# A two-layer decoder trunk on one core: the relative bias table is built in the first mixer instead of the first feed-forward

## The chip, the cores and the metric

The kernel runs on one core of one Trainium2 chip. The time is device microseconds (us) from the launch to the end on that core; a median over several runs is compared with a median. Beside the timed runs one execution was taken with the hardware profiler, and all rows below are from that one.

## The reference

The program computes two layers of a decoder on 256 tokens of width 1024. Each layer is a half-step feed-forward, a mixer and a second half-step feed-forward; every sub-layer is modulated by shift, scale and gate vectors made from a conditioning vector `c` and the weights `w_ada`.

```python
for l in range(DEPTH):                                   # DEPTH = 2
    mod = (silu(c) @ w_ada[l] + b_ada[l]).reshape(...)   # 9 vectors of 1024 per layer
    h = pre(x, 0)                                        # RMS norm, scale, shift
    x = x + 0.5 * mod[:, 0, 2] * swiglu(h, w_ffn_gate[l, 0], w_ffn_up[l, 0], w_ffn_down[l, 0])
    h = pre(x, 1)
    q_sb, ..., g_swa = split(h @ w_in[l])
    o_sb  = stick_breaking_mixer(q_sb, k_sb, v_sb)       # uses no bias
    o_dil = dilated_mixer(q_dil, k_dil, v_dil, rel_bias) # scores + band_bias(rel_bias)
    o_swa = swa_mixer(q_swa, k_swa, v_swa, rel_bias, sinks[l])
    merged = sigmoid(g_sb) * (o_sb @ w_br_sb[l]) + ...   # three gated branches
    x = x + mod[:, 1, 2] * (merged @ w_out[l])
    h = pre(x, 2)
    x = x + 0.5 * mod[:, 2, 2] * swiglu(h, ...)
return rmsnorm(x, final_gain)
```

The part that matters here is the bias: for each of 12 softmax heads, each query row needs the bias of its distance to every key, masked where the head may not look. The table `rel_bias` is 32 buckets by 12 heads and is the same for both layers.

## The kernel before

The stages run in the order FFN 0, mixer 1, FFN 2, FFN 3, mixer 4, FFN 5. All weights stream from HBM once. Work goes in **units**, each a 128x1024 piece of weights (half of a 1 MB `raw` tile). For each unit ScalarE (ACT) rounds the piece to a high part (`wH`, line 150), VectorE (DVE) makes the low part by subtracting (`wL`, line 158), and TensorE (PE) multiplies with both parts. `feed` keeps this splitting five units ahead of PE (`AHEAD = 5`, six buffers of each part, three `raw` buffers). An FFN has 44 units of gate and up products (FFN 0 begins with 12 in another form, so 32 in its loop; tile `pf`), then 22 units of down products (`pd`), the last four in pieces. After them come the gate and residual on DVE (`y`, `x`, lines 535 and 536), a norm, and transposes (`psn`) for the next stage. A mixer has 6 units of value products (`pv`), 14 units of query and key products (`pq`), then gates and branches (`pg`, `pb`), then the output rows.

Between the units a second stream runs: 512 KB pieces of `w_ada` (tile `ada`, two buffers) are multiplied and summed on DVE (`acc`, line 283), a few per unit by a written table of paces. Nothing is reordered by a scheduler: every engine runs its instructions in the order in which the code issues them, and so does each queue. All weight loads are issued on SP's queue (`q1` in the profile) in program order; each waits there for its buffer.

Attention in the mixer is interleaved with units. The stick-breaking pairs (no bias) run beside the query and key units: scores on PE (`pz`) behind unit 5, `z` on DVE, three activations into `e`, `e` again on DVE beside unit 7 (line 986), cumulated sums on PE (`pc`) behind unit 9, `z` minus them on DVE (line 995), an exponential, and the product `po` behind unit 11. The softmax heads start with the first gate unit; there the bias tile `Tm` is added to the scores on DVE (line 1054).

The bias is made in three helpers: four small loads on SP's queue; one small fp32 product, a masked sum and two DMAs on POOL's queue (`q0` in the profile); and one load per mixer, which reads the repeated rows at a slant so that each query row gets its own shift.

```python
def bias_loads(self):                      # line 413
    nc.sync.dma_start(oh, a["onehot"]); nc.sync.dma_start(mk, a["dmask"])
    nc.sync.dma_start(rb, a["rel_bias"]); nc.sync.dma_start(self.sink, a["sinks"]...)
def bias_table(self):                      # line 425
    nc.tensor.matmul(p[:NHEAD, :NDIST], rb, oh, start=True, stop=True)          # psr
    nc.vector.tensor_tensor(mk, p[:NHEAD, :NDIST], mk, op=ALU.add)
    nc.gpsimd.dma_start(row, mk)                                                # 12x383 to DRAM
    nc.gpsimd.dma_start(self.scr, row.unsqueeze(1).to_broadcast([NHEAD, P, NDIST]))
def load_bias(self, T):                    # line 435
    nc.gpsimd.dma_start(T, src)                                                 # scr to SBUF
```

Below, "the copy" is the second DMA of `bias_table` (`scr<-row`, DRAM to DRAM, 1536 rows of 383 floats).

Of the kernel before, what the change touches and what calls it, by code (L numbers as in the profile page):

```python
# [89 lines left out]
class Trunk:  # L90
# [704 lines left out]
    def run_ffn(self, plan, early=None):  # L795
        s = plan["s"]
        if s:
            self.alloc_ffn(s)
        if s:
            us = plan["in"][:2]  # L800
            for u in us:
                self.feed()
                self.ada_tick()
                u.pe(u, "high")
            for u in us:
                u.pe(u, "low")
            self.done(2)
        for i, u in enumerate(plan["in"]):
            if i > 1 or s == 0:
                self.step(u)  # L810
            if s == 0 and i == 8:
                self.bias_loads()
            if s == 0 and i == 16:
                self.bias_table()
        self.flush()
        self.run_rows(plan["out"], s, self.ffH, self.ffL, early)

# [320 lines left out]
    def run_mixer(self, plan):  # L1138
        s, l = plan["s"], plan["l"]
        nc = self.nc  # L1140
        bigA = self.sp.tile([P, 5376], F32, tag="bigA", name=f"qkv{s}", bufs=1)
        self.qk = bigA[:, 0:3840].rearrange("p (b n) -> p b n", n=S)
        self.v = bigA[:, 3840:5376].rearrange("p (t n) -> p t n", t=2)
        bigB = self.sp.tile([P, 5120], F32, tag="bigB", name=f"Tm{s}", bufs=1)
        self.T = bigB[:, 0:3072].rearrange("p (h n) -> p h n", n=256)
        self.m = bigB[:, 3072:5120].rearrange("p (b n) -> p b n", n=S)
        self.oH = self.sp.tile([P, 6, S], F32R, tag="oA", name=f"oH{s}", bufs=1)
        self.oL = self.sp.tile([P, 6, S], F32R, tag="oB", name=f"oL{s}", bufs=1)
        self.load_bias(self.T)

        pv = plan["pv"]
        for i, u in enumerate(plan["v"]):
            self.feed()
            self.ada_tick()
            self.v_pe(i, u, pv, (1,) if i < 2 else (0, 1), "high" if i < 2 else "all")
            if i == 1:
                for k in range(2):
                    self.v_pe(k, plan["v"][k], pv, (1,), "low")
                self.done(2)
            elif i > 1:  # L1160
                self.done()
        for t in range(2):
            self.v_post(t, pv[t])

        sb, soft = self.sb_stages(s), self.soft_stages(s, l)
        when = {}

        def at(part, fns, arg, units):
            for fn, i in zip(fns, units):
                if fn:  # L1170
                    when.setdefault((part, i), []).append((fn, arg))

        at("qk", sb, 0, (5, 6, 7, 9, 10, 11))
        at("qk", sb, 1, (7, 8, 9, 11, 12, 13))
        at("br", soft[:4], ("dil", 0), (0, 1, 2, 4))
        at("br", soft[:4], ("dil", 1), (2, 3, 4, 6))
        at("br", soft[4:], "dil", (8,))
        at("br", soft[:4], ("swa", 0), (7, 8, 9, 11))
        at("br", soft[:4], ("swa", 1), (10, 11, 12, 15))
        at("br", soft[4:], "swa", (17,))  # L1180
        for i, u in enumerate(plan["qk"]):
            self.step(u)
            if i == 4:
                nc.scalar.preload_act_table_set("natural_log_exp_and_others")
            for fn, arg in when.get(("qk", i), ()):
                fn(arg)
        nc.scalar.preload_act_table_set("exp_and_others")
        for i, u in enumerate(sum(plan["br"], [])):
            if i == len(plan["br"][0]) + len(plan["br"][1]):
                mm = self.sp.tile([P, 2, KB, S], F32R, tag="bigA", name=f"mHL{s}", bufs=1)  # L1190
                self.mH, self.mL = mm[:, 0], mm[:, 1]
            self.step(u)
            for fn, arg in when.get(("br", i), ()):
                fn(arg)
        self.flush()
        self.run_rows(plan["out"], s, self.mH, self.mL)
# [154 lines left out]
```

## Time and profile before

| | |
|---|---|
| median of 3 runs | 1212.38 us (1212.31 to 1213.13) |
| the profiled execution | 1215.12 us, of which its span is 1213.4 us |
| PE busy | 1181.0 us, 97% of the span |
| DVE busy | 837.3 us, 69% |
| ACT busy | 616.0 us, 51% |
| mean granted PE clock | 0.992 of full speed |
| DMA | 287.55 MB, mean 237 GB/s |

A busy share is a mean over stages with different limits, and PE's ends are modelled, so a stretch can count as busy although matmuls in it stand further apart. What a stage is bound by is read from the chain of work that ended last and from the waits of that stage.

### The profile page before, as it was taken

The numbers are of one execution on the slowest core, as the hardware profiler recorded it, in microseconds if no ns is written. First come the engines' busy times: TensorE is split into PE (matmuls) and PEld (weight loads), VectorE is DVE, ScalarE is ACT, GpSimd is POOL, SyncE is SP. The second block draws the span as 40 slices with busy tenths as digits, with TensorE's granted clock in tenths as the row PEclk, the third lists the DMA queues.
The fourth block names the chain that finished last, engine by engine and source line by source line (L and its number), as shares of the span: only waits on it lengthen the run. The fifth ranks groups of instructions, "written<-read, shape, count | busy, mean of one in ns | idle before, by whom it ended". The sixth has DMA issues, their size and how long they took to land.

```text
span 1213.4 us, 21101 instructions
## 1 busy us (share of the span) xinstructions
PE 1181.0 (97%) x8765; PEld 1102.9 (91%) x8765; DVE 837.3 (69%) x1087; ACT 616.0 (51%) x953; POOL 19.0 (2%) x38
## 2 busy tenths in 40 slices
PE   6999998899999999999999999999999999999997
PEld 5999986699999899999889999889999998999986
DVE  3677575878889888766577666567766788555544
ACT  5555343556555475444365444346655456444432
POOL 1000000000000000000000000000000000000000
PEclk9999999899999999999999999999999999999999
DMA  9999889698769959876738676748743584556550
GB/s 318 313 303 332 272 308 318 211 314 271 253 230 314 319 176 326 263 243 242 261 112 298 219 242 226 258 157 291 264 149 113 186 276 147 190 178 197 180 176 35
DMA packets 189671, 287.55 MB, mean 237 GB/s; under 512 B 6806, under 2 KB 155496, under 8 KB 189576
## 3 DMA queue, kind: packets, MB, share of 16 engines
q1 hardware_dynamic: 187656, 279.88, 68.8%
q0 software_dynamic: 1776, 6.14, 1.7%
q8 instruction: 68, 1.11, 0.4%
q14 instruction: 27, 0.22, 0.1%
q10 hardware_dynamic: 144, 0.20, 0.0%
HBM read 285.12 MB, written 3.42 MB: 238 GB/s over the span
## 4 chain that ended last, share of the span: by engine, by line
PE 85%; DMA 6%; DVE 3%; ACT 2%; issue 2%; POOL 1%; SPq 0%; POOLq 0%; ACTq 0%; DVEq 0%
PE pf L594 37%; PE pd L706 16%; PE pg L594 12%; PE pq L594 7%; DMA ada<-in_w_ada 5%; PE pb L594 3%; PE pf L624 3%; PE pv L942 2%; DVE acc L283 1%; DVE wL L158 1%; PE adaf L212 1%; DMA first<-in_w_ada 1%; PE psn L488 1%; ACT wH L150 1%; ACT jk L452 0%
## 5 line engine op out<-in xcount | busy, mean ns | idle before, releaser
L158 DVE TENSOR_TENSOR wL<-raw,wH 128x1024 fp32r<-128x1024 f32 (+1 forms) x384 | 461.8, 1211 | 224.8 <-ACT wH L150 224.3
L150 ACT CAST wH<-raw 128x1024 fp32r<-128x1024 f32 (+1 forms) x384 | 393.1, 1040 | 244.5 <-PE pd L706 90.1
L594 PE MATMUL pf<-hH,wH 128*128 128x256 f32 x1312 | 324.5, 285 | 0.4 <-DVE hH L505 0.4
L594 PE MATMUL pf<-hH,wL 128*128 128x256 f32 x1312 | 323.5, 284 | 0.0
L594 PEld LDWEIGHTS pf<-hH,wH 128*128 128x128 f32 x1312 | 253.1, 193 | 1.7 <-issue 0.9
L594 PEld LDWEIGHTS pf<-hH,wL 128*128 128x128 f32 x1312 | 253.5, 193 | 0.2 <-issue 0.2
L594 PE MATMUL pf<-hL,wH 128*128 128x256 f32 x1312 | 183.8, 283 | 0.0
L283 DVE SCALAR_TENSOR_TENSOR acc<-ada,sc,acc 128x1024 f32<-128x1024 f32 x112 | 143.4, 1280 | 40.6 <-DMA ada<-in_w_ada 40.6
L594 PEld LDWEIGHTS pf<-hL,wH 128*128 128x128 f32 x1312 | 169.1, 192 | 0.0
L706 PE MATMUL pd<-wL,ffH 128*128 128x512 f32 x336 | 132.7, 395 | 5.1 <-DVE wL L158 5.1
L706 PE MATMUL pd<-wH,ffH 128*128 128x512 f32 x336 | 132.5, 394 | 0.0
L706 PE MATMUL pd<-wH,ffL 128*128 128x512 f32 x336 | 132.2, 393 | 0.0
L594 PE MATMUL pg<-hH,wH 128*128 128x256 f32 x384 | 96.0, 288 | 0.0
L594 PE MATMUL pg<-hH,wL 128*128 128x256 f32 x384 | 94.0, 283 | 0.0
L652 ACT ACTIVATE sil<-pf 128x256 f32<-128x256 f32 x88 | 33.3, 382 | 98.4 <-PE pf L594 98.4
L706 PEld LDWEIGHTS pd<-wL,ffH 128*128 128x128 f32 x336 | 63.9, 190 | 19.3 <-DVE wL L158 6.2
L706 PEld LDWEIGHTS pd<-wH,ffH 128*128 128x128 f32 x336 | 63.9, 190 | 14.0 <-issue 0.8
L706 PEld LDWEIGHTS pd<-wH,ffL 128*128 128x128 f32 x336 | 64.0, 190 | 13.2
L594 PEld LDWEIGHTS pg<-hH,wH 128*128 128x128 f32 x384 | 73.5, 191 | 2.3 <-issue 0.9
L594 PEld LDWEIGHTS pg<-hH,wL 128*128 128x128 f32 x384 | 73.6, 192 | 0.0
L653 DVE TENSOR_TENSOR f<-pf,sil 128x256 f32<-128x256 f32 x88 | 36.9, 422 | 33.9 <-ACT sil L652 33.9
L594 PE MATMUL pq<-hH,wH 128*128 128x256 f32 x224 | 55.8, 287 | 0.0
(215 smaller groups left out, 1437.2 us busy)
## 6 DMA issues: line engine op xcount, KB each, us to landing
ada<-in_w_ada SPq DMA_DIRECT2D x128, 512.0 KB, 5.4
raw<-in_w_ffn_down SPq DMA_DIRECT2D x44, 1024.0 KB, 4.8
raw<-in_w_in SPq DMA_DIRECT2D x42, 1024.0 KB, 6.1
raw<-in_w_ffn_gate SPq DMA_DIRECT2D x41, 1024.0 KB, 6.1
raw<-in_w_ffn_up SPq DMA_DIRECT2D x41, 1024.0 KB, 5.8
first<-in_w_ada SPq DMA_DIRECT2D x32, 256.0 KB, 6.0
raw<-in_w_out SPq DMA_DIRECT2D x8, 1024.0 KB, 7.1
raw<-in_w_ffn_gate SPq DMA_DIRECT2D x12, 256.0 KB, 6.0
```

The costliest lines, as they stand in the source:

```text
L150: nc.scalar.copy(u.H, u.view(self.raw_tiles[u.raw]))
L158: nc.vector.tensor_tensor(u.L, u.view(self.raw_tiles[u.raw]), u.H, op=ALU.subtract)
L212: self.nc.tensor.matmul(self.first_ps[q % 2][32 * i:32 * i + 32, 0:P], w, src[:, i * P:(i + 1) * P], start=kb in (0, None), stop=kb == KB - 1)
L283: self.nc.vector.scalar_tensor_tensor(acc, src, sc, acc, ALU.mult, ALU.add)
L488: self.nc.tensor.transpose(p[:, i * P:(i + 1) * P], xn[:, fb * P:(fb + 1) * P], self.ident)
L594: nc.tensor.matmul(out, w[:, kb, cs], x[:, kb, :], start=i == 0, stop=i == n - 1)
L624: self.nc.tensor.matmul(ps[fb][:, S * up:S * up + S], w[:, 2 * k + up, b * P:(b + 1) * P], x[:, 2 * q + k, :], start=q == 0 and not up and ...
L652: nc.scalar.activation(sil, p[:, :S], AF.Silu)
L653: nc.vector.tensor_tensor(f32, p[:, S:], sil, op=ALU.mult)
L706: self.nc.tensor.matmul(out, x[:, kb, sl], w[:, 0, hs], start=first and i == 0, stop=last and i == 2)
L942: self.nc.tensor.matmul(out, x[:, 4 * (i % 2) + k, sl], w[:, k, :], start=i % 2 == 0 and j == 0, stop=i % 2 == 1 and j == n - 1)
```

## The change

The four small loads and the table are no longer issued behind units 8 and 16 of FFN 0's loop. In the first mixer the loads are issued at its start in the place of `load_bias`, and the table and then `load_bias` behind the last value unit (i = 5). The second mixer is as before. No instruction is added or left out.

```diff
@@ run_ffn
         for i, u in enumerate(plan["in"]):
             if i > 1 or s == 0:
                 self.step(u)
-            if s == 0 and i == 8:
-                self.bias_loads()
-            if s == 0 and i == 16:
-                self.bias_table()
         self.flush()
@@ run_mixer
-        self.load_bias(self.T)
+        if s == 1:
+            self.bias_loads()
+        else:
+            self.load_bias(self.T)
 
         pv = plan["pv"]
         for i, u in enumerate(plan["v"]):
...
                 self.done(2)
             elif i > 1:
                 self.done()
+            if s == 1 and i == 5:
+                self.bias_table()
+                self.load_bias(self.T)
         for t in range(2):
             self.v_post(t, pv[t])
```

On SP's queue of the kernel before, the four small loads stand between the weight loads of FFN 0 (`in_w_ffn_gate`, `in_w_ffn_up`).

```order
L133 DMA raw_1066<-in_w_ffn_up 128x8x256
L260 DMA ada_1069<-in_w_ada 128x1024
L418 DMA oh<-in_onehot 32x383
L419 DMA mk<-in_dmask 12x383
L420 DMA rb<-in_rel_bias 32x12
L422 DMA sink<-in_sinks 128x12
L133 DMA raw_1139<-in_w_ffn_gate 128x8x256
```

In the changed kernel they stand behind the third weight load of the query and key units (`in_w_in`).

```order
L133 DMA raw_2255<-in_w_in 128x8x256
L133 DMA raw_2457<-in_w_in 128x8x256
L133 DMA raw_2465<-in_w_in 128x8x256
L418 DMA oh<-in_onehot 32x383
L419 DMA mk<-in_dmask 12x383
L420 DMA rb<-in_rel_bias 32x12
L422 DMA sink<-in_sinks 128x12
L133 DMA raw_2513<-in_w_in 128x8x256
```

They moved past all weight loads of FFN 0's second half. On POOL's queue of the kernel before, the row and the copy stand ahead of the norm of FFN 0's end (`r`), and the load of the bias tile behind it.

```order
L431 DMA row<-mk 12x383
L433 DMA scr<-row 1536x1x383
L466 TENSOR_TENSOR r_0_2311<-ms_0_2287 128x1
L467 TENSOR_TENSOR r_0_2311<-r_0_2311,mhalf 128x1
L467 TENSOR_TENSOR r_1_2427<-r_1_2427,mhalf 128x1
L439 DMA Tm_2485<-scr 128x12x256
```

In the changed kernel all three stand behind that norm, one after the other.

```order
L466 TENSOR_TENSOR r_0_2296<-ms_0_2272 128x1
L467 TENSOR_TENSOR r_0_2296<-r_0_2296,mhalf 128x1
L467 TENSOR_TENSOR r_1_2412<-r_1_2412,mhalf 128x1
L431 DMA row<-mk 12x383
L433 DMA scr<-row 1536x1x383
L439 DMA Tm_2470<-scr 128x12x256
```

So the load of the bias tile now waits for the copy, which is issued just ahead of it. On PE of the changed kernel the small product stands between the last value unit and the first query unit.

```order
L938 MATMUL pv_1_1_2387<-wL_2463,hH_2337 128x256
L938 MATMUL pv_1_1_2387<-wH_2459,hL_2338 128x256 x4
L428 MATMUL psr<-oh,rb 12x383
L594 MATMUL pq_0_2646<-hH_2337,wH_2505 128x256
L594 MATMUL pq_0_2646<-hH_2337,wL_2509 128x256
```

Before, it stood between two units of FFN 0, `pf_14` and `pf_15`; here the first query unit has to wait until it is done.

## Rows read from the trace of the kernel before

**Rows 1.** Windows: busy us (instructions) PE, PEld, DVE, ACT, POOL, clock, DMA share, GB/s.

```profile
116.30:140.40 24.10, 24.10 (x193) 23.14 (x193) 14.38 (x18) 8.80 (x14) 1.12 (x1) 1.00 0.94 261
160.00:180.00 20.00, 20.00 (x95) 15.94 (x95) 13.45 (x15) 9.62 (x11) 0.00 (x0) 1.00 0.88 295
258.00:282.00 24.00, 24.00 (x201) 23.41 (x200) 18.42 (x22) 14.90 (x18) 0.00 (x0) 1.00 0.92 306
282.00:295.00 13.00, 13.00 (x107) 11.80 (x106) 9.57 (x11) 7.76 (x11) 0.00 (x0) 1.00 0.62 214
```

**Rows 2.** The chain that ended last: start us, us, what.

```profile
109.61 0.74 PE psr L428 x2
...
124.33 19.39 DMA ada<-in_w_ada
...
222.44 0.61 DVE y L535
...
227.99 1.27 PE psn L488 x8
...
252.64 17.28 PE pq L594 x144
...
283.50 0.43 PE pc L992 x2
...
753.18 57.15 PE pd L706 x252
...
812.12 1.10 PE psn L488 x8
```

**Rows 3.** DMA issues: KB each, us from issue to landing.

```profile
Tm<-scr POOLq DMA_DIRECT2D x2, 1536.0 KB, 7.8
...
scr<-row POOLq DMA_DIRECT2D x1, 2298.0 KB, 24.1
...
oh<-in_onehot SPq DMA_DIRECT2D x1, 47.9 KB, 7.5
...
row<-mk POOLq DMA_DIRECT2D x1, 18.0 KB, 4.8
...
rb<-in_rel_bias SPq DMA_DIRECT2D x1, 1.5 KB, 7.0
```

**Rows 4.** DMA queues in 112 to 142 us: packets, MB, share of 16 engines.

```profile
q1 hardware_dynamic: 3709, 5.93, 62.8%
q0 software_dynamic: 736, 2.37, 30.5%
```

**Rows 5.** Waits of DVE in 112 to 146 us: us, times, longest.

```profile
DVE acc L283 <- DMA ada<-in_w_ada: 10.2, 2, 6.2
```

**Rows 6.** Timeline of DVE: start us, us, instruction, idle before it.

```profile
124.92 1.23 DVE L158 TENSOR_TENSOR wL<-raw,wH 128x1024 fp32r<-128x1024 f32 x1 [0.28 <-ACT wH L150]
...
161.89 1.23 DVE L158 TENSOR_TENSOR wL<-raw,wH 128x1024 fp32r<-128x1024 f32 x1 [0.52 <-ACT wH L150]
...
212.30 1.22 DVE L158 TENSOR_TENSOR wL<-raw,wH 128x1024 fp32r<-128x1024 f32 x1
```

**Rows 7.** Timeline of PE: a unit of `pf` and the first matmul of `pd`.

```profile
123.59 0.28 PE L594 MATMUL pf<-hH,wH 128*128 128x256 f32 x1
...
155.27 0.40 PE L706 MATMUL pd<-wH,ffH 128*128 128x512 f32 x1
```

**Rows 8.** Waits of PE in 186 to 228 us.

```profile
PE pd L706 <- DVE wL L158: 5.1, 2, 4.4
```

**Rows 9.** DMA queues in 228 to 244 us, as in rows 4.

```profile
q0 software_dynamic: 400, 1.57, 30.6%
```

**Rows 10.** Timeline of SP's queue at the mixer's start.

```profile
244.35 0.37 SPq L133 DMA_DIRECT2D raw<-in_w_in  x1
...
247.82 0.37 SPq L133 DMA_DIRECT2D raw<-in_w_in  x1
```

**Rows 11.** Timeline of DVE in mixer 1, as in rows 6.

```profile
278.94 0.95 DVE L986 SCALAR_TENSOR_TENSOR e<-z,e 128x768 f32<-128x768 f32 x1
...
306.97 0.68 DVE L1054 SCALAR_TENSOR_TENSOR p_dil<-pa_dil,Tm 128x512 f32<-128x512 f32 x1
```

**Rows 12.** Waits of PE in 240 to 405 us, all of them.

```profile
PE pv L942 <- DVE wL L158: 0.6, 1, 0.6
```

## The prediction

> **What bounds the kernel now.** I read the chain of work that ended last first. Nearly everywhere it is PE going from product to product, with one long exception: from 124.33 us, in FFN 0, it is a load of `ada` of 19.39 us, and from there to DVE's `y` at 222.44 it stays on `ada` loads, DVE and ACT [rows 2]. The reader should see there that FFN 0's second half is not PE's: it ends when its loads let DVE finish. How much PE loses is read by setting FFN 0's end beside FFN 3's, which the chain shows as PE alone: from the first `pd` matmul to the transposes 812.12 - 753.18 = 58.9 us [rows 2]. FFN 0 starts `pd` at 155.27 [rows 7] and has its transposes at 227.99 [rows 2], 72.7 us. So 13.8 us are lost there; only 5.1 us of it are listed as a wait of `pd` for the low parts [rows 8], since the rest stands before `y`.
>
> Then the windows. In 116.3 to 140.4 us, while the copy is under way, the DMA engines are 0.94 busy and move 261 GB/s [rows 1]: 6.29 MB, of which 2.37 are the copy's queue [rows 4]. SP's queue is left with 3.92 MB, 163 GB/s; it has 295 soon after [rows 1]. In mixer 1 PE waits for 0.6 us in all [rows 12], so PE is the bound there, but the loads are close behind it: 306 GB/s at 0.92 of the engines in 258 to 282 us, with a lull (0.62) only behind that [rows 1].
>
> **What leaves FFN 0.** The four small loads, the product (0.74 us of PE [rows 2]), the row and the copy. The copy is what counts: 30.5% of a window of 30 us on 16 engines [rows 4] is 9.15 us of the whole DMA. What it did to DVE is a measured row: DVE, which is in order, stood 10.2 us in two waits for `ada` [rows 5]. Part of that is caught up before it matters. The split of a unit is issued five units before PE reaches it, so the split at 124.92 belongs beside the unit that PE began at 123.59: 1.3 us late [rows 6, 7]. I count 11 splits from it to the one at 161.89, and as many units of PE up to the first `pd` matmul; that one belongs at 155.27: 6.6 us late [rows 6, 7]. So the copy leaves 5.3 us. After that, 15 more units take 212.30 - 161.89 = 50.4 us [rows 6], 3.36 us each, where PE needs 57.15/252 x 12 = 2.72 [rows 2]: the loads set this pace with the copy long gone, so it stays, and nothing more is caught up or lost. Then `y` moves from 222.44 to about 217.1 and the transposes to 222.7; PE alone could be there at 155.27 + 58.9 = 214.2, so it does not cap this. **Gain 5.3 us.** Bounds: 3, if DVE would have been late at 155 us anyway by the small delays of a busy queue (2 us, as much again as the 1.3 seen); 9.15, if all the DMA time that is freed comes back.
>
> **What enters mixer 1.** The small loads go out behind the load at 244.35, and the next waits for its buffer until 247.82 [rows 10], so their issue (four in about 2 us) fits between and moves nothing. They must land before PE ends the value units at 252.6, where the first `pq` stands in the chain [rows 2]. Issued at 244.7 and 245.8, with 7.5 and 7.0 us to landing [rows 3], `oh` is there at 252.2 and `rb` at 252.8. I take a wait of 0.3 us of PE; 0 to 2 by how full the queue is. Behind PE's product wait the first query unit and, on DVE, the sum and the next split, which DVE reaches at about the same time. The product itself costs its 0.74 us in full, since PE has no idle time here. **Loss 1.0 us.**
>
> The row is issued at about 254.5 and lands 4.8 us later [rows 3]; the copy goes out at 259.3 and, at 24.1 us [rows 3], lands at 283.4. The load of the bias tile follows at once and takes 7.8 us [rows 3] or more. It takes 30.6% of 16 us, 4.9 us of the whole DMA [rows 9], and used to run while nothing else did. Neither is waited for by the scores: the first use of the tile is at 306.97 [rows 11], over 10 us after even a landing at 295. What they do is take DMA from SP's queue, on which `ada` and the weights of the query units come. SP's queue moved 306 GB/s there [rows 1] and is left with 163 if the copy takes what it took before: (1 - 163/306) x 24.1 = 11.3 us of lateness. The same sum for FFN 0, with 295, gives 10.8 where DVE's row has 10.2 [rows 5], so I take 10.2. DVE reaches the first stick-breaking `e` at 278.94 and ends it at 279.9 [rows 11]; PE takes it up at 283.50 [rows 2]. That slack of 3.6 us is the only cover: the five units of splits ahead help the weights and not this exchange, which goes PE, DVE, ACT, DVE, PE. Late by 10.2 us, `e` is ready at 290.1 and PE stands 6.6 us. The load of the tile comes on top: nothing if it fits into the lull behind 282 us (0.38 x 13 = 4.9 us free [rows 1], just its size), up to 4.9 us if it hits the same loads, so 6.6 to 11.5. Catching up works the other way: in FFN 0 the 10.2 had shrunk to 5.3 some 20 us after the copy; here `e` comes only 7 us of work after, so a third of that, 1.6, and with the lateness down to 7 the least would be 3.4. I take 9.0, the middle of 6.6 and 11.5, because DVE's position at the copy's end (old 273) lies before the lull. What is late next is `z` minus the sums and then `po`; they move with PE, and later time is not won back, as PE is without idle time to the end of the mixer. **Loss 9.0 us, 3.4 to 11.5.**
>
> How two queues share the engines is the weakest point. In 112 to 142 us they took 62.8% and 30.5% [rows 4], so the copy had 9.15/24.1 = 0.38 of the engines while it ran.
> [...] By an even share of time the copy would have taken 18.3 us and DVE would lose 9.2 us instead of 10.2, and the sum below would be 1.0 us lower; the trace shows a slower copy and SP's queue at little more than half its rate, which is nearer to even than to free.
>
> **The sum.** -5.3 + 1.0 + 9.0 = +4.7 us. On the profiled execution: span 1213.4 to 1218.1, its time 1215.12 to 1219.8. That one ran 2.7 us over the median of the runs, 1212.38; I carry the difference over: **1217.1 us**.
>
> **Rivals.** (A) *The mixer absorbs it.* The lateness at `e` stays under 3.6 us, which needs the copy to take less of the engines than before or SP's queue to have enough loaded ahead. For it: DVE waits in FFN 0 came with a queue already behind, and 0.62 in 282 to 295 is real room. Against it: 14 us of DMA work (9.15 + 4.9) meet 0.08 x 24 + 4.9 = 6.9 us of room in 258 to 295 [rows 1]. It ends faster: -5.3 + 0.74 + 0 to 2 gives 1208 to 1210. (B) *The two cancel*: late splits cost PE 4 to 6 us, FFN 0 gives 5 to 7; 1210 to 1214.8. (C) *FFN 0 gives nothing*: its end is set by the pace of `ada` (3.36 us a unit) and 10.2 us of DVE's waiting would have come later anyway. For it, the 50 us behind 161.89 run at that pace whatever came before; against it, a shift of their start shifts their end. With 9 to 10 lost: 1222. A wait of the softmax heads for the tile is no case of its own, with over 10 us to spare.
>
> **Chances.** The forecast 0.50 (1214.8 to 1220.5), A 0.22, B 0.17, C and worse 0.11. Slower by over 0.2% (2.4 us, about what a measurement of this kernel can tell from no change) are the forecast and C, 0.61; within it is B, 0.17; faster is A, 0.22. The range for 8 in 10 reaches down through A and up to C: 1208 to 1222.
>
> **What would show it.** Right: no load of `ada` near 19 us in FFN 0, `y` some 5 us earlier; in mixer 1 waits of PE for `e` or `z` (`pc`, `po`) of 7 to 12 us in all that are not there now, DVE waiting for `ada` by some 10 us more in 258 to 295 us, the copy still near 24 us. Wrong: PE without waits in mixer 1 (A), `y` unmoved (C), a wait of PE for the softmax scores (the tile late after all), or a wait of the product for its small loads of several us, which would come on top.

## The result and the profile after

The changed kernel takes 1225.79 us (median of 4 runs, 1222.11 to 1226.3) where the kernel before takes 1212.35 beside it (4 runs): 1.0104 of it, 95% interval 1.009 to 1.0118. It is slower, as forecast, but by 13.4 us where 4.7 were forecast, and outside the range. The profiled execution took 1226.3 us, at the upper end of its runs; its span is 11.2 us longer than the one of before.

The page of the changed kernel, its span and its first part (busy us, share, instructions): the busy times are those of before within 1.7 us, so in sum PE stands idle 11.6 us longer (span less busy time: 44.0 us against 32.4).

```profile
span 1224.6 us, 21097 instructions
...
PE 1180.6 (96%) x8765; PEld 1102.9 (90%) x8765; DVE 838.3 (68%) x1087; ACT 617.7 (50%) x953; POOL 18.9 (2%) x38
```

The chain of the changed kernel from FFN 0's end to the first gate unit (start us, us, what). In FFN 0 it has no `ada` load of 19 us any more; `y` stands at 215.92, where before had 222.44 [rows 2]. The chain's longest load, again of 19 us, stands in mixer 1 now, at 260.70. PE is out of the chain from 231.64 until `pc` at 293.38; in the kernel before it was back in it at 240.97.

```profile
215.92 0.61 DVE y L535
...
221.45 1.97 PE psn L488 x8
223.42 1.92 PE pe L706 x9
225.34 2.54 PE adag L344 x4
...
230.75 0.89 PE psn L488 x8
...
252.59 6.70 DMA ada<-in_w_ada
...
259.39 1.30 DVE acc L283
...
260.70 19.14 DMA ada<-in_w_ada
...
279.93 1.30 DVE acc L283
...
281.24 8.60 DMA ada<-in_w_ada
...
291.14 1.22 DVE wL L158
292.36 0.88 DVE e L982
...
293.38 1.19 PE pc L988 x2
...
297.13 3.55 PE pq L594 x24
...
301.24 3.06 PE pq L594 x24
```

PE's waits in mixer 1 (who, for whom: us in all, times, longest) were 0.6 us in all [rows 12]. Now, in 235 to 425 us (the third line is of the stage's first products and stood before too, with 0.6 us ahead of 240 us, where the window of [rows 12] begins):

```profile
PE pc L988 <- DVE e L982: 13.1, 1, 13.1
PE pv L938 <- DVE wL L158: 0.6, 1, 0.6
PE pv L938 <- DVE hL L525: 0.5, 1, 0.5
```

DVE's waits in 250 to 295 us, in the same form, first of the kernel before, then of the changed one. In 112 to 146 us, where the copy ran before and DVE lost 10.2 us [rows 5], there is no wait for `ada` now. In mixer 1 there were 7.9 us already, so 13.4 us are new there.

```profile
DVE acc L283 <- DMA ada<-in_w_ada: 7.9, 4, 3.4
```

```profile
DVE acc L283 <- DMA ada<-in_w_ada: 21.3, 4, 10.5
```

The queues while the copy runs, 254 to 277 us (packets, MB, share of 16 engines), and the loads issued there (KB, us to landing). The copy takes 22.7 us (24.1 before [rows 3]) and SP's queue moves 4.13 MB in 23 us, 180 GB/s.

```profile
q1 hardware_dynamic: 2695, 4.13, 55.9%
q0 software_dynamic: 704, 2.36, 37.5%
...
scr<-row POOLq DMA_DIRECT2D x1, 2298.0 KB, 22.7
raw<-in_w_in SPq DMA_DIRECT2D x2, 1024.0 KB, 19.1
ada<-in_w_ada SPq DMA_DIRECT2D x3, 512.0 KB, 12.8
```

Windows of the changed kernel (us; busy us and count of PE, PEld, DVE, ACT, POOL; granted clock, DMA share, GB/s). After each of the two stretches in which PE stands, its granted clock is at 0.50, also while the next products run (222 to 225 us, 293 to 296 us).

```profile
216.00:219.00 3.00, 1.09 (x10) 0.88 (x8) 2.93 (x6) 1.05 (x3) 0.00 (x0) 1.00 1.03 384
219.00:222.00 3.00, 0.55 (x3) 0.55 (x4) 2.90 (x6) 1.72 (x5) 1.09 (x2) 0.67 0.74 244
222.00:225.00 3.00, 3.00 (x16) 3.00 (x15) 1.52 (x6) 2.68 (x10) 0.00 (x0) 0.50 0.01 2
225.00:228.00 3.00, 3.00 (x9) 1.49 (x9) 2.05 (x4) 1.50 (x4) 0.00 (x0) 0.69 0.02 5
...
284.00:287.00 3.00, 0.00 (x0) 0.00 (x0) 1.74 (x4) 2.29 (x3) 0.00 (x0) 0.65 0.97 363
287.00:290.00 3.00, 0.00 (x0) 0.00 (x0) 0.06 (x1) 1.17 (x2) 0.00 (x0) 0.50 0.95 329
290.00:293.00 3.00, 0.00 (x0) 0.00 (x0) 3.00 (x3) 1.84 (x3) 0.00 (x0) 0.50 0.44 131
293.00:296.00 3.00, 2.62 (x8) 2.36 (x9) 3.00 (x7) 2.37 (x3) 0.00 (x0) 0.50 0.76 286
296.00:299.00 3.00, 3.00 (x17) 2.93 (x16) 1.73 (x2) 2.97 (x5) 0.00 (x0) 0.58 0.73 212
299.00:302.00 3.00, 3.00 (x30) 2.46 (x29) 3.00 (x5) 1.01 (x2) 0.00 (x0) 1.00 0.57 196
```

Stage by stage between the two profiles (us):

| stretch | before | after | difference |
|---|---|---|---|
| to the first `pd` matmul | 155.27 | 154.18 | -1.1 |
| from there to `psn` | 72.7 | 67.3 | -5.4 |
| `psn` to the last value unit's end | 24.65 | 26.95 | +2.3 |
| the small product `psr` | | 0.74 | +0.7 |
| first `pq` to `pc` | 30.86 | 44.22 | +13.4 |
| `pc` to the first gate unit | 17.77 | 20.44 | +2.7 |
| the rest | | | -1.4 |

A stretch is good to some 0.2 us, since a product can be counted from its own start or from the end of the one before it, which overlap (before, `adag` starts at 230.17 and the product ahead of it ends at 230.33). The rest lies almost all in FFN 5, which no instruction of the change touches; it is no part of the result.

### The profile page after: what moved, and what is told of

Read it like the earlier page. It is cut to its first block, busy times and chain, and to the rows that moved or that the text cites. A ratio compares the mean times of both kernels' runs of the same rounds, so it can differ in the third digit from the quotient of the medians.

```text
span 1224.6 us, 21097 instructions
## 1 busy us (share of the span) xinstructions
PE 1180.6 (96%) x8765; PEld 1102.9 (90%) x8765; DVE 838.3 (68%) x1087; ACT 617.7 (50%) x953; POOL 18.9 (2%) x38
## 4 chain that ended last, share of the span: by engine, by line
PE 84%; DMA 8%; DVE 3%; ACT 2%; issue 2%; POOL 1%; SPq 0%; POOLq 0%; ACTq 0%; DVEq 0%
PE pf L594 39%; PE pd L706 17%; PE pg L594 11%; DMA ada<-in_w_ada 5%; PE pq L594 4%; PE pb L594 3%; PE pf L624 2%; PE pv L938 1%; DMA first<-in_w_ada 1%; DVE acc L283 1%; DVE wL L158 1%; PE psn L488 1%; DMA raw<-in_w_in 1%; ACT jk L452 0%; DMA raw<-in_w_ffn_up 0%
## 5 line engine op out<-in xcount | busy, mean ns | idle before, releaser
L706 PEld LDWEIGHTS pd<-wL,ffH 128*128 128x128 f32 x336 | 63.1, 188 | 14.6 <-DVE wL L158 2.0
L706 PEld LDWEIGHTS pd<-wH,ffH 128*128 128x128 f32 x336 | 63.1, 188 | 13.8 <-issue 0.8
L706 PEld LDWEIGHTS pd<-wH,ffL 128*128 128x128 f32 x336 | 63.1, 188 | 13.2
```

What stands on the lines that cost most here:

```text
L706: self.nc.tensor.matmul(out, x[:, kb, sl], w[:, 0, hs], start=first and i == 0, stop=last and i == 2)
```

## The experiments

Theory M: the copy takes DMA from SP's queue, `ada` loads come late, DVE (in order) comes late to `e`, PE waits; FFN 0 gains what it is rid of; and each opened wait costs a few us more by PE's clock. Rivals are named with each run. Ratios are to the kernel before, run beside it, with 95% intervals.

**The parts of the change.** Three runs took it apart. First the load of the tile alone was moved in the code, with loads, table and copy left in FFN 0:

```diff
@@ run_mixer
-        self.load_bias(self.T)
+        if s != 1:
+            self.load_bias(self.T)
...
+            if s == 1 and i == 5:
+                self.load_bias(self.T)
```

> The table is made and copied in FFN 0 as in the kernel before; only the load of the bias tile goes to the end of the first mixer's value units. Theory (the copy takes DMA from SP's queue, the loads of w_ada come late, DVE with them, and PE waits for e): the load is 4.9 us of DMA work, DVE gets 3 to 5 us late, the slack of 3.6 us at e covers most of it: PE waits 0 to 1.5 us there, time 1212 to 1214. Rival (the load of the tile is the dear part, the copy is absorbed): PE waits over 5 us, time over 1217.

1212.97 us (10 runs), 1.0007 [0.9998, 1.0016]. The run told nothing on the question. Nothing on POOL's queue makes that load wait, so it went out as early as ever, by POOL's timeline at 233.30 us (234.29 before):

```profile
233.30 1.09 POOL L439 DMA_DIRECT2D Tm<-scr  x1 [0.29 <-issue]
```

The second run kept the change and put the load of the tile behind query unit 11:

```diff
             if s == 1 and i == 5:
                 self.bias_table()
-                self.load_bias(self.T)
...
+            if s == 1 and i == 11:
+                self.load_bias(self.T)
```

> As the changed kernel, but the load of the bias tile is issued behind the twelfth query and key unit, when PE has passed the wait for e. Theory: PE still waits about 10 us for e (13.1 less the 3 us by which the tile's load lengthens the last load of w_ada in that stretch), the copy still takes about 23 us, time 1221 to 1224. Rival (the tile's load is the dear part): PE waits under 4 us, time under 1216.

1224.32 us (4 runs), 1.0098 [1.0082, 1.0113], with a wait of 12.6 us for `e`. A miss for the same reason: the load left at 274.53, as soon as the copy had landed. In effect this was the changed kernel once more.

The third left the copy out of the kernel before and filled the tile from another tensor, so the softmax heads get numbers that are not the bias:

```diff
         nc.gpsimd.dma_start(row, mk)
-        self.scr = ...
-        nc.gpsimd.dma_start(self.scr, row.unsqueeze(1).to_broadcast([NHEAD, P, NDIST]))
...
-        src = bass.AP(...)
+        src = self.a["w_out"][0]...[:, 0:NHEAD, :]
         self.nc.gpsimd.dma_start(T, src)
```

> The kernel before without the copy from DRAM to DRAM; the bias tile is filled from another tensor at the same place, so the softmax heads get numbers that are not the bias. It shows what the copy costs FFN 0. Theory: FFN 0's transposes come 6.5 us earlier as in the changed kernel, of which 2.3 us are given back because PE works at half its clock after the wait ahead of them: time 1207.5 to 1209. Rival 1 (the half clock is no cost of this place): 1205.5 to 1206.5. Rival 2 (FFN 0's end is set by the pace of the loads, not by the copy): 1211 to 1212.5.

1209.6 us (7 runs), 0.9973 [0.9962, 0.9985]: 1.8 to 4.6 us faster; the time is just above the theory's range and outside both rivals'. In its profile `y` is at 214.92, 7.5 us earlier, but the first `pq` at 247.37 only 5.3 us earlier. This bounds what any place of the copy outside FFN 0 can give.

**The copy against SP's queue, without the change.** A second copy was put into mixer 4 of the kernel before, to a second scratch in DRAM that nobody reads, and held on POOL until the values are there:

```diff
+        if s == 4:
+            hold = self.work([P, 1], "hold", "hold", 1)
+            nc.gpsimd.tensor_tensor(hold, self.v[:, 0, 0:1], self.v[:, 0, 0:1], op=ALU.add)
+            scr2 = ...
+            nc.gpsimd.dma_start(scr2, self.row.unsqueeze(1).to_broadcast([NHEAD, P, NDIST]))
```

> The kernel before with one copy more: behind the second mixer's value units the row is copied once again, into a second scratch that nobody reads, held on POOL's queue until the values stand in SBUF. FFN 0 and mixer 1 are as before. In mixer 4 the kernel before ends the first e at 862.4 and needs it at 868.2 us, a slack of 5.9 us, and has about half as many loads of w_ada beside the query and key units. Theory (the copy halves SP's rate whatever the stage): DVE gets 8 to 10 us late, PE waits 2 to 5 us for e or z, and less than 1 us more by its clock: 1214 to 1218. Rival 1 (only a stage with as many loads of w_ada as mixer 1 is hit): PE waits nothing, within 1 us of before. Rival 2 (what was dear in mixer 1 is the table's chain or its place, not the copy): the same as rival 1.

1218.45 us (6 runs), 1.0051 [1.0033, 1.0068]; the profiled execution was the longest of the six, 1223.23. The copy went out at 837.05 and took 23.2 us. PE's waits in that mixer, and below the chain there:

```profile
PE pc L992 <- DVE e L986: 6.2, 1, 6.2
```

```profile
840.76 21.81 DMA ada<-in_w_ada
...
873.29 0.88 DVE e L986
874.16 0.14 issue
874.30 1.19 PE pc L992 x2
```

The same chain in a place that the change does not touch (with 5 `ada` sums between the first `pq` and `e`, where mixer 1 has 7; that is more than the half expected), with a bit more than the theory's 2 to 5 us of wait, and with PE's clock at 0.50 in 873 to 876 us here too. The copy alone, with no load of the tile behind it and FFN 0 unchanged, makes the wait.

**The load of the tile.** In the first run the table stays in FFN 0, and the load is held on POOL until query unit 0 is copied, so that it goes out at 258.09:

```diff
-        self.load_bias(self.T)
+        if s != 1:
+            self.load_bias(self.T)
...
+            if s == 1 and i == 1:
+                hold = ...
+                nc.gpsimd.tensor_tensor(hold, self.qk[:, 0, 0:1], self.qk[:, 0, 0:1], op=ALU.add)
+                self.load_bias(self.T)
```

> The run t_only changed nothing: POOL's queue waits for nothing there, so the load went out at 233 us as before. Here the table and the copy stay in FFN 0, and the load of the bias tile is held on POOL's queue by a one-column sum that reads what the first pair of query units leaves, so that it goes out at about 259 us among the weight loads. Theory: 4.9 us of DMA work make DVE 2 to 5 us late against a slack of 3.6 us: PE waits 0 to 2 us for e, time 1212 to 1214. Rival (the tile's load is a dear part of the 13.1 us): a wait over 4 us, time over 1216.

1214.91 us (10 runs), 1.0014 [1.0003, 1.0026]; PE waits 1.3 us for `z` and 0.7 for `e`. Alone the tile's 4.9 us of DMA mostly go into the slack.

The other is the changed kernel with the load held to query unit 10 (out at 299.33, behind the first `pc`):

```diff
-                self.load_bias(self.T)
...
+            if s == 1 and i == 11:
+                hold = ...
+                nc.gpsimd.tensor_tensor(hold, self.qk[:, 10, 0:1], self.qk[:, 10, 0:1], op=ALU.add)
+                self.load_bias(self.T)
```

> The run copy_only changed nothing for the same reason. Here the changed kernel's tile load is held on POOL's queue until the copy of the twelfth query unit, about 303 us, behind the wait for e; it must land by about 317 us. Theory: the wait for e falls from 13.1 us by the 2 to 4 us by which the tile's load lengthens the last load of w_ada ahead of it, to 9 to 11 us, and PE's half clock behind it stays: 1221 to 1224. Rival (the tile's load decides): the wait falls under 6 us. A second price could come in: the tile late for the first softmax scores, seen as a wait of DVE or PE there.

1224.04 us (4 runs), 1.009 [1.0071, 1.0108]. PE's waits in mixer 1:

```profile
PE pc L988 <- DVE e L982: 8.3, 1, 8.3
PE pt_dil L1104 <- DVE p_dil L1085: 2.0, 1, 2.0
```

The wait for `e` falls from 13.1 to 8.3, more than the theory's 2 to 4 us and less than the rival's 7: of the changed kernel's wait 4.8 us are the tile's and 8.3 the copy's (the copy itself took 20.6 us in this run and 22.7 in that one, and a second profile of the changed kernel has 12.5 us of wait, so the split is good to about a microsecond). In time little comes back; part of it turns into a wait of the softmax heads, for which the tile now comes late.

**Without `ada` loads in the query units.** Both kernels with a table of paces that takes most of those loads out of the stretch and puts them behind it:

```diff
-PACE = (..., (0, 1.5, 1.5, 1, 0.75, 0.75), ...
+PACE = (..., (0, 0.4, 2, 1.5, 1.25, 1.25), ...
```

> The changed kernel with other paces for the loads of w_ada in mixer 1: 0.4 instead of 1.5 beside the query and key units, more beside the gates, branches and output rows (as many in all). To be read against before_pace, which has the same paces. Theory (the link from the copy to PE is the load of w_ada, for which DVE waits in order behind the weight loads of the same queue; the weights themselves are loaded ahead by five units): with a quarter of those loads there, DVE's wait for w_ada ahead of e falls from 21 to under 8 us and PE's wait for e from 13 to 0 to 3 us; the changed kernel is then 0 to 4 us faster than before_pace. Rival (the weights are late as such, any DMA work there delays DVE): PE still waits 8 us and more for e, and the changed kernel stays over 5 us slower than before_pace.

> The kernel before with the same paces as after_pace; the control. No wait of PE for e; more work of DVE beside the gates and branches, where it is over 90% busy, may cost PE some us there: 1211 to 1218. Both theories expect the same of it.

The changed kernel took 1237.51 us (4 runs), 1.0209 [1.0193, 1.0225]; the control 1239.65 (4 runs), 1.0235 [1.0217, 1.0254]. The control's time was far from what I expected: this pace costs 27.8 us behind the query units, so only the pair says something. In it the change is not slower any more (2.1 us less by the medians, with overlapping intervals). DVE's waits in 250 to 298 us with the change:

```profile
DVE wL L158 <- ACT wH L150: 18.1, 9, 6.0
DVE oL L1013 <- ACT oH L1012: 2.3, 1, 2.3
DVE z L969 <- PE pz L965: 1.4, 1, 1.4
```

DVE waits for the weights instead of `ada`, which the five units ahead cover, and PE does not wait for `e` at all, although the copy (18.7 us) ran at the same place. From the first `pq` to the end of `e` it takes 30.0 us, against 26.4 in the control, whose slack there is 4.5 us; in the changed kernel it takes 44.1 against 27.4 before. So it is the `ada` loads through which nearly all of the copy's delay reaches `e`; some 3.6 us come without them.

**The copy where the DMA is idle.** In the kernel before SP's queue moves almost nothing in 228 to 236 us (0.03 MB). The copy was split from the table and put on POOL's queue behind the first half of the norm of FFN 0's end:

```diff
@@ end of FFN 0
             xn0 = self.norm_x(0, s + 1)
+            if s == 0:
+                self.bias_copy()
...
```

> As the kernel before, but the copy alone is taken out of FFN 0's middle and issued on POOL's queue behind the first half of the norm at FFN 0's end (220 to 227 us), where the DMA engines stand idle until about 237 us; loads, product, row and the tile's load stay where they were. Theory: FFN 0 gains what the run without the copy gained, 2.4 to 4 us; the copy runs alone and needs 10 to 13 us; the tile's load follows it and overlaps 3 to 6 us with the weights of the value and query units, in which DVE is ahead: no wait of PE for e over 1 us, time 1208 to 1211. Rival (any DMA work between FFN 0 and the query units comes back as a wait there): a wait for e of 3 us and more, time 1212 and over.

1212.68 us (12 runs), 1.0001 [0.9991, 1.0011], no gain where 2 to 4 us were expected. The copy went out at 218.94 and needs 16.1 us although it runs nearly alone (SP's queue holds 4.7% of the engines in 219 to 235.2 us), so the load of the tile leaves only at 235.55 and meets the weights of the query units: PE waits 2.0 us for `e`. Next the load of the tile was held to query unit 8 as well (out at 281.50), and then 16 products of constants were put on PE ahead of the transposes:

```diff
+            if s == 1 and i == 9:
+                hold = ...
+                nc.gpsimd.tensor_tensor(hold, self.qk[:, 8, 0:1], self.qk[:, 8, 0:1], op=ALU.add)
+                self.load_bias(self.T)
```

> As copy_idle (the copy at FFN 0's end), and the tile's load held on POOL's queue until the copy of the tenth query unit, about 283 us, into the lull of the loads there. Theory: the wait of 2.0 us for e that copy_idle had goes, since no second queue runs beside the weights of the query units until then; the tile lands at 292 to 295, ahead of its first use at about 302: 1208.5 to 1211, faster than before by 2 to 4 us. Rival (the gain at FFN 0's end is used up by the copy there, in the norm or in the value units' weights): no faster than before, 1211.5 to 1214.

> As idle_late, with 16 small matmuls of constants ahead of the transposes at FFN 0's end. Theory: the granted clock stays at 1.00 there and 1.5 to 2.3 us more come back: 1206.5 to 1209.5. Rival (the extra matmuls delay the transposes by as much): the same as idle_late.

1210.74 us (11 runs), 0.999 [0.9978, 1.0003], with no wait for `e`; and 1210.37 (11 runs), 0.9988 [0.9979, 0.9997]. Both are misses: 1.2 us less than before where 2 to 4 were expected, and 0.4 us more by the products where 1.5 to 2.3 were. The second is the only version with the whole computation that is faster than before, by 0.12%: within what counts as no change here.

**PE's clock.** Products of constants, which nobody reads, keep PE busy in the two waits: 16 ahead of the transposes, 52 ahead of `pc`.

```diff
+    def warm(self, n, name):
+        p = self.ps(name)
+        for i in range(n):
+            self.nc.tensor.matmul(p[:, 0:P], self.ones, self.tri, start=True, stop=True)
...
+            self.warm(16, "warm0")
...
+                self.warm(52, "warm1")
```

> The changed kernel with 16 small matmuls of constants ahead of the transposes at FFN 0's end and 52 ahead of the first cumulated sums of mixer 1, where PE waits; nothing reads their results. Theory (PE's clock falls to half because it stands idle, and work behind the wait then runs slowly): the granted clock stays at 1.00 there, 2.3 + 2.7 us come back, time 1220 to 1222. Rival (the slower stretch has another cause, or these matmuls only add to the path): time the same as the changed kernel's or up to 4 us over it.

1221.99 us (4 runs, 1219.63 to 1225.2), 1.008 [1.0056, 1.0103]. In its profile the clock is 1.00 in all windows of 3 to 4 us in 204 to 240 and 280 to 305 us; from `psn` to `psr` it takes 24.6 us (26.95 without) and from `psr` to the first gate unit 63.1 (65.4). Then each alone, beside the changed kernel again:

> The changed kernel as it is, as the control of the two runs beside it: 1222 to 1227, ratio to before about 1.010.

> The changed kernel with the 52 small matmuls ahead of the first cumulated sums of mixer 1 alone. Theory (the idle wait lowers PE's clock and the work behind it pays 2.7 us): the clock stays at 1.00 behind the wait, 2 to 3 us less than after_again in the same call. Rival (the clock's fall costs nothing in the time of whole runs): within 1 us of after_again.

> The changed kernel with the 16 small matmuls ahead of the transposes at FFN 0's end alone. Theory: the clock stays at 1.00 there and about 2 us come back against after_again, unless they are swallowed by the wait for e in mixer 1, whose loads start earlier by as much and so keep the gain: 1.5 to 2.3 us less. Rival: within 1 us of after_again.

The changed kernel gave 1224.12 us (5 runs), 1.0093 [1.008, 1.0106]; with the mixer's wait filled 1222.15 (4 runs), 1.0078 [1.0065, 1.0091]; with the norm's filled 1223.0 (6 runs), 1.008 [1.0067, 1.0094]. Windows with the mixer's wait filled:

```profile
284.00:287.00 3.00, 3.00 (x29) 3.00 (x29) 0.00 (x0) 1.78 (x2) 0.00 (x0) 1.00 0.99 340
287.00:290.00 3.00, 3.00 (x29) 3.00 (x29) 2.49 (x3) 1.23 (x2) 0.00 (x0) 1.00 0.68 226
290.00:293.00 3.00, 2.40 (x18) 2.13 (x17) 3.00 (x7) 2.41 (x4) 0.00 (x0) 1.00 0.86 284
293.00:296.00 3.00, 3.00 (x32) 2.75 (x30) 1.73 (x2) 2.97 (x5) 0.00 (x0) 1.00 0.68 218
296.00:299.00 3.00, 3.00 (x30) 2.70 (x23) 3.00 (x5) 1.01 (x2) 0.00 (x0) 1.00 0.58 208
```

With work added in the mixer the median is 2.0 us lower, though the intervals overlap; in the profile the stretch from `pc` to the first gate unit is 2.1 us shorter (18.3 against 20.4 in the changed kernel's second profile). Ahead of the norm the medians give 1.1 us here, between the theory's 1.5 to 2.3 and the rival's less than 1, and 0.4 us in the run before: a gain in time is not shown there. In the profiles the clock stays at 1.00 there, and `psn` to `psr` takes 24.6 us instead of 26.5.

## Why the direction was right and the size wrong

**FFN 0: right, a little small.** The split that stood at 161.89 [rows 6] stands at 156.71, 5.2 us earlier; 5.3 were counted. The 15 units behind it take 48.8 us (205.49 - 156.71) where before took 50.4, so their pace stays set by the loads, as was argued against the rival in which FFN 0 gives nothing. `y` and the transposes come 6.5 us earlier, 1.2 more than counted. That the counted split agrees to 0.1 us is partly luck: the splits around it are 5.2 to 9 us earlier and most behind it 6.4 to 7.2. Of this, 1.1 us stand ahead of the copy already (the split at 124.92 is at 123.82 now): the sum charged the product's 0.74 us to the mixer and did not credit FFN 0 with them. One pair of profiles is a thin base, but others agree: in five with FFN 0 as before `y` stands at 218.3 to 222.4, in eight of the changed kernel and its variants at 213.4 to 215.9.

**The small loads: right.** The product costs its 0.74 us; `oh` and `rb` landed in 6.1 and 5.3 us and PE did not wait for them (0.3 taken).

**The mixer's wait: right mechanism, at the right place, too small.** It came at `pc` for `e`, behind `ada`, with no wait of the softmax heads: 13.1 us where 9.0 were taken and 11.5 was the upper bound. Two terms were mis-sized. The copy's own share was put at 10.2 - 3.6 = 6.6 and is 8.3. With the slack of 3.6 that is a lateness of 11.9. The prediction had 11.3 from SP's rate in the mixer and chose FFN 0's row instead, then allowed for catching up, of which nothing is seen. But with the rate measured now the same sum gives only (1 - 180/306) x 22.7 = 9.3, and the slack is one execution's: in the profiles of the first run and of the copy in mixer 4, which leave mixer 1 as before, `e` ends 2.1 and 0.7 us ahead of `pc`. Whether the lateness or the slack was mis-sized stays open. The rows of the latter:

```profile
280.53 0.95 DVE L986 SCALAR_TENSOR_TENSOR e<-z,e 128x768 f32<-128x768 f32 x1
```

```profile
282.19 0.59 PE L992 MATMUL pc<-e,tri 128*128 128x256 f32 x2
```

The load of the tile was put between 0 and 4.9 us and its middle taken; it costs 4.8, the whole of its DMA time. The lull behind 282 us did have the room: in 277 to 288 us the tile took 43.3% of the engines beside 47.1% of SP's queue. But the last `ada` load ahead of `e` was under way in it and took 8.60 us; with the tile held back the chain has no load of `ada` between the sum at 278.24 and `e` at 285.39, and DVE waits 15.4 us for `ada` in 250 to 298 us where it waited 21.3. So the one load that DVE waits for decides, and not the mean room. Together 9.0 + 1.7 + 2.4 = 13.1. The share of the engines was not what failed: the copy had 37.5% (38% taken), and SP's queue 180 GB/s where 163 were taken. A single `ada` load stood 19.14 us in the chain; that this is the queue's order, with 1 MB weight loads ahead of it and two `ada` buffers only, was not tried apart.

**The step that is missing: PE's clock.** The prediction priced each wait by its length. But PE stood 4.4 us ahead of `psn` and 13.1 us ahead of `pc`, and came out of both at 0.50: `psn` took 1.97 us instead of 1.27, `adag` 2.54 instead of 1.72, a query unit 3.55 where before shows 2.86 (rows below). By the stretches this is 2.3 and 2.7 us, 5.0 in the profiles. In whole runs it is less: both waits filled give 1.0080 of the kernel before, where the changed kernel has 1.0104 and 1.0093, so 2 to 3 us, with overlapping intervals. The kernel before has such a fall too, in 212 to 221 us of its trace, but there PE was held up by late splits anyway (5.1 us in two waits for `wL` [rows 8]). So in this profile a part of FFN 0's gain is lost again at once: of 6.5 us 4.2 are left. The fall ahead of the norm is not the change's alone: in the run with only the tile's load held, FFN 0 is as before, and yet PE stands 4.9 us there and the next stretch is 2.2 us longer. The rows of the kernel before, in the forms used above:

```profile
218.00:221.00 3.00, 3.00 (x8) 2.33 (x8) 1.45 (x2) 1.90 (x2) 0.00 (x0) 0.50 0.90 266
```

```profile
230.33 1.72 PE adag L344 x4
...
285.26 2.86 PE pq L594 x24
```

The sum should have had a term for it: the trace of before shows the clock at 0.50 behind the longer of those two waits, 4.4 us [rows 8].

With these, in the profiles: -6.5 + 0.7 + 13.4 + 5.0 = +12.6 us, less the 1.4 of the rest, is the 11.2 of the spans. Against the forecast's 4.7 that is 1.2 less by FFN 0, 0.3 less by the small loads, 4.4 more by the mixer's wait, 5.0 more by the clock and 1.4 less by the rest. The medians differ by 13.4 and 12.2 us in the two comparisons; the 1 to 2 us above 11.2 the two profiles do not show, and the one of the kernel before ran 2.7 us over its median.

**The rivals.** That the mixer absorbs it falls: PE waits 13.1 us, not under a slack of 3.6. That the two cancel falls with it. That FFN 0 gives nothing falls too, by the 6.5 us and by the run without the copy; its time of 1222 came nearest to the result, for another reason.

## What to carry to other kernels

Price a moved DMA by who waits, in order, on the queue that it competes with (here DVE on `ada`, 13.4 us more than before), and by the slack of the tightest exchange between engines behind that (3.6 us), not by when the moved data is first used. Compare that slack over several executions: it was 0.7 to 3.6 us here. Give each long wait that opens on PE a term for the slow products behind it (here 2.3 and 2.7 us in the profiles behind 4.4 and 13.1 us of wait, in whole runs 2 to 3 us for both, with overlapping intervals). To place a DMA in time, look at what its queue waits for: here the load of the tile left at 233.30 us with its line behind the last value unit, and at 274.53, when the copy had landed, with its line behind query unit 11; it left at 258.09 and 299.33 where a sum ahead of it on that queue had to wait.

## What was not expected of the hardware

The copy is slow by itself: with hardly any other traffic it took 15.4 to 16.5 us in the three kernels that run it behind FFN 0, 2.36 MB in rows of 1532 bytes, and in the first of them it held 58.3% of the engines and SP's queue 4.7%. So, by an estimate from these times, its 21 to 24 us beside the weights are made by sharing only for a third or so. And products of constants in a wait kept PE's clock at 1.00 and made the stretch behind it 2.1 us shorter in the profile of the mixer; the medians of whole runs are 2.0 us apart.
